# Key and query scratch with the two rows of a map side by side

## The chip, the cores and the metric

The kernel runs on one core of a Trainium2 chip. The metric is the device time of one execution in microseconds (us). The profile shows a single execution, with the instructions of five engines: TensorE (PE, with its weight loads as PEld), VectorE (DVE), ScalarE (ACT), GpSimd (POOL) and SyncE (SP). SP computes nothing here. It issues nearly all transfers between memory and the chip's buffers (DMAs), in one order; ACT issues the weight loads of some stages. The transfers themselves run on the core's 16 DMA engines.

## The reference

Two layers, each with a mixer of three parallel head groups and a feed-forward part, run over 1024 latent tokens and 128 context tokens (1152 columns in all; the keys of the cache add 128). The change touches one of the head groups, the differential attention with 4 heads of two maps each:

```python
def block(qi):
    s = jnp.einsum('bqhmd,bkhmd->bhmqk', qi, k).astype(jnp.float32) * scale
    p = jax.nn.softmax(s, axis=-1)
    w = p[:, :, 0] - lam * p[:, :, 1]
    return jnp.einsum('bhqk,bkhe->bqhe', w.astype(v.dtype), v)
```

The other two groups, a gated DeltaNet and an mLSTM, are recurrences over chunks of the sequence, in both directions. Queries and keys of the latent tokens go through a rotary embedding, in which a pair of channels (x0, x1) becomes (x0 cos - x1 sin, x0 sin + x1 cos).

## The kernel before

Activations lie with channels on the 128 partitions and tokens along the rows, in three groups of 384 columns. Everything is float32; a number is split into a rounded part and a rest (h and l), and a product is three matmuls (`mm3`, L189 to L191), in the attention's scores two (L1250).

Each layer has three stages. In **w_in** the input projections run and their results go to scratch in memory (`open_s`, L430 on). `blk_a` computes queries and keys: two projection blocks, p = 0 and p = 1, hold the first and the second channel of all rotary pairs, 4 maps x 32 channels on the partitions. After the rotary step `put` splits the result in h and l and stores it, by `put_q` in QD and by `put_k` in KD. Beside it `prep1`, `inverse` and `prep2` prepare the recurrences (`prep2` loads ND by the tile w, L851, and stores into RD from X, L911).

In **mixers** the attention (`attention`, L1211 on) and the two recurrences (`scan`) are interleaved on all engines. For each head the attention loads two K tiles, one for a map, 128 partitions x 1280 columns (L1228), and V (L1231). A K tile holds on its partitions h and l of both channels of the pairs: (h or l, p, 32 channels). For each 256 queries it loads one Q tile (L1236) by two DMAs, one for each half of the partitions, because the queries are needed against h and against l of the keys. Then L1250 multiplies (two matmuls into a PSUM bank, for the h and the l part of the queries), L1251 scales and takes the maximum on DVE, L1256 takes the exponential on ACT. K has three buffers, V and Q two. The recurrences load rd, vr, qk, rm, v1 and cq for each step (L1051 to L1149). All these loads are issued by SP, in one order, which the framework that builds the program arranges, with the instructions of all engines, by a simulated timeline; on the chip each engine then works through its own list in order. So a DMA issue that is held up holds up all issues behind it, of the recurrences too.

The third stage is the output projection and the feed-forward part; its weights are loaded by ACT. No line of it is changed.

The layout of the scratch decides what a DMA looks like from the memory's side. Before, QD is `[8, 2, 64, NT]` (map, h or l, 32p + channel, token) and KD is `[2, 2, 2, P, NT + P]` (half, h or l, p, 4 maps x 32 channels, token). A store into QD takes 4 maps x 32 channels, so its outer loop counts 4, and h and l are two DMAs. A load of K takes (h or l, p) x 32 channels, so its outer loop counts 4 too.

Of the kernel before, what the change touches and what calls it, by code (L numbers as in the profile page):

```python
# [9 lines left out]
F32 = mybir.dt.float32  # L10
# [7 lines left out]
P = 128  # L18
# [4 lines left out]
NT = NL + NC  # L23
# [47 lines left out]
class Kern:  # L71
# [362 lines left out]
    def open_s(self, l):  # L434

        S = self.S = {}
        dt = lambda n, shape: self.dr.tile(shape, F32, name=f"{n}{l}")
        S["BT"] = dt("BT", [P, 6, CVO])
        S["CQK"] = dt("CQK", [P, 4, NT])
        S["V1"] = dt("V1", [NCH, P, H, 65])  # L440
        S["BC"] = dt("BC", [NCH, P, 512])
        S["QD"] = dt("QD", [8, 2, 64, NT])
        S["KD"] = dt("KD", [2, 2, 2, P, NT + P])
        S["VD"] = dt("VD", [10, P, 512])
        S["ND"] = dt("ND", [2, NCH, P, H, P])
        S["RD"] = dt("RD", [2, NCH, P, 1024])
        S["GR"] = dt("GR", [2, 16, NT])
        S["VK"] = dt("VK", [NCH, P, 768])
        S["RM"] = dt("RM", [2, NCH, P, 768])
        S["CAT"] = dt("CAT", [KB, P, NT])  # L450
        ed, pe = ExitStack(), ExitStack()
        self.dn = ed.enter_context(self.pool("psdn", PSUM))
        self.pp = pe.enter_context(self.pool("pspp", PSUM))
        return ed, pe
# [472 lines left out]
    def put(self, dst, src, w):  # L927

        t = self.t(self.pr, [P, 2, GW], "kh", 2, F32R)[:, :, :w]
        self.nc.scalar.copy(t[:, 0], src)  # L930
        self.nc.vector.tensor_sub(t[:, 1], src, t[:, 0].bitcast(F32))
        if len(dst) == 1:
            self.nc.sync.dma_start(dst[0], t.bitcast(F32))
        else:
            for i in range(2):
                self.nc.sync.dma_start(dst[i], t[:, i].bitcast(F32))

    def put_k(self, hf, p, cols, src, w):
        self.put([self.S["KD"][hf, :, p, :, cols].rearrange("l r t -> r l t")], src, w)

    def put_q(self, hf, p, cols, src, w):
        self.put([self.S["QD"][4 * hf:4 * hf + 4, hl, 32 * p:32 * p + 32, cols] for hl in range(2)], src, w)

    def blk_a(self, l, qk, hf, u):

# [265 lines left out]
    def attention(self, l):  # L1211

        nc, S, at, pa = self.nc, self.S, self.at, self.pa
# [9 lines left out]
        for h in range(H):  # L1223
            K = []
            for m in range(2):
                k = self.t(at, [P, NT + P], "K", 3, F32R)
                r = 64 * (h % 2) + 32 * m
                nc.sync.dma_start(k.bitcast(F32), S["KD"][h // 2].rearrange("l p r t -> (l p) r t")[:, r:r + 32, :])  # L1228
                K.append(k)
            V = self.t(at, [P, 10, 128], "V", 2)  # L1230
            nc.sync.dma_start(V, S["VD"][:, :, 128 * h:128 * h + 128].rearrange("s p e -> p s e"))  # L1231
            for q0 in range(0, NT, 256):
                nq = min(256, NT - q0)
                q = self.t(at, [P, 2, 2, 256], "Q", 2, F32R)
                for hh in range(2):
                    nc.sync.dma_start(q[64 * hh:64 * hh + 64, :, :, :nq].bitcast(F32), S["QD"][2 * h:2 * h + 2, :, :, q0:q0 + nq].rearrange("m l p t -> p m l t"))  # L1236
                ctx = q0 >= NL
                kt = [9] if ctx else list(range(9))
                groups = [kt] if ctx else [kt[0:3], kt[3:6], kt[6:9]]
# [1 line left out]
                for j in range(nq // 128):  # L1241
                    es, zs = [], []
                    for m in range(2):
                        e = self.t(at, [P, NT], "e", 4)
                        mx = self.t(at, [P, 4], "mx", 4)
                        for i, ks in enumerate(groups):
                            w = 128 * len(ks)
                            p = self.ps(pa, "s", 2)
# [24 lines left out]
                    for i, ks in enumerate(groups):  # L1273
                        n = len(ks)
                        p = self.ps(pa, "t", 1)
# [278 lines left out]
```

## Time and profile before

| | |
|---|---|
| median of 3 runs | 3792.35 us (3791.3 to 3798.47) |
| the profiled execution | 3797.68 us |
| its span, first to last instruction | 3795.9 us, 59415 instructions |
| mean granted TensorE clock in it | 0.954 of full speed |
| DVE, ACT, POOL busy | 2295.8, 1136.6, 654.4 us |
| moved by DMA | 434.13 MB, 277091 packets |

Busy time is the time in which an engine has an instruction of its own under way. A busy PE can still be waiting inside the pipeline, so it is not PE at its peak; but an idle PE is idle. The view of waits tells, for each engine and line, how long the engine was idle just before it, how often, and what released it. The timeline gives instructions in order of time; in it, a bracket holds the idle time of the engine before the instruction and the releaser. Times count from the start of the span. The first layer's mixers run from about 547 to 955 us, the second layer's from about 2425 to 2830 us.

### The profile page before, as it was taken

The page shows a single profiled execution, that of the slowest core. Times are in us where ns is not written, and L with a number is a line of the kernel's source. Part 1 is how long each engine was busy: PE and PEld are TensorE (multiplying, and loading weights), DVE is VectorE, ACT ScalarE, POOL GpSimd, SP SyncE. Part 2 cuts the span into 40 slices and gives each one's busy share as a digit, 9 for nine tenths or more (in the row PEclk, how much of TensorE's full clock was granted, in tenths as well). Part 3 has the DMA queues.
Part 4 walks back from the last instruction along what each step waited for, and adds up shares of the span by engine and source line. Part 5 has one row for each costly group of instructions (what it writes and reads, how often), then busy time and mean ns, then how long its engine had stood idle before and what let it go on. Part 6 is the DMA issues. An engine that isn't in the chain of part 4 may idle for free. (4 is left out here: it accounts for less than half of the span.)

```text
span 3795.9 us, 59415 instructions
## 1 busy us (share of the span) xinstructions
PE 3540.6 (93%) x22770; PEld 3369.8 (89%) x22770; DVE 2295.8 (60%) x5361; ACT 1136.6 (30%) x2383; POOL 654.4 (17%) x903
## 2 busy tenths in 40 slices
PE   7999978997899999999999997898789999999998
PEld 6997777886899999999989877788778999999997
DVE  7896677787455566654485567477775434333435
ACT  5323315445241111111243431244553311111111
POOL 2014232355020000000020324034632000000001
PEclk8999988999999999999999999889999999999999
DMA  5377624774212222221133663467542111111111
GB/s 215 128 247 234 217 78 124 225 214 132 92 59 84 78 81 81 95 78 48 59 110 99 221 230 97 132 175 205 137 140 66 34 39 41 49 40 39 51 45 56
DMA packets 277091, 434.13 MB, mean 114 GB/s; under 512 B 24648, under 2 KB 186504, under 8 KB 276552
## 3 DMA queue, kind: packets, MB, share of 16 engines
q1 hardware_dynamic: 247576, 324.29, 27.3%
q10 hardware_dynamic: 29232, 106.05, 8.7%
q8 instruction: 180, 2.95, 0.3%
q14 instruction: 103, 0.84, 0.1%
HBM read 315.85 MB, written 114.39 MB: 113 GB/s over the span
## 5 line engine op out<-in xcount | busy, mean ns | idle before, releaser
L362 DVE SCALAR_TENSOR_TENSOR x<-pd,mod,x 128x256 f32<-128x256 f32 (+1 forms) x832 | 405.2, 514 | 597.5 <-PE pd L191 596.3
L183 ACT CAST wh<-wr 128x1024 fp32r<-128x1024 f32 (+1 forms) x219 | 229.1, 1047 | 880.3 <-PE pu L190 462.2
L184 DVE TENSOR_TENSOR wl<-wr,wh 128x1024 fp32r<-128x1024 f32 (+1 forms) x219 | 267.6, 1228 | 173.6 <-ACT wh L183 173.1
L189 PE MATMUL pd<-hh,wh 128*128 128x384 f32 x1056 | 358.8, 340 | 7.3 <-DVE x L362 5.1
L189 PE MATMUL pg<-uh,wh 128*128 128x384 f32 x1056 | 357.2, 338 | 2.6 <-ACT uh L342 2.6
L190 PE MATMUL pg<-ul,wh 128*128 128x384 f32 x1056 | 357.9, 339 | 1.4 <-DVE ul L347 1.4
L299 POOL TENSOR_TENSOR nacc<-nacc,nsq 128x384 f32<-128x384 f32 x48 | 52.1, 1086 | 1769.6 <-issue 1572.7
L190 PE MATMUL pu<-ul,wh 128*128 128x384 f32 x1056 | 355.7, 337 | 0.0
L189 PE MATMUL pu<-uh,wh 128*128 128x384 f32 x1056 | 355.6, 337 | 0.0
L190 PE MATMUL pd<-hl,wh 128*128 128x384 f32 x1056 | 354.9, 336 | 0.0
L191 PE MATMUL pg<-uh,wl 128*128 128x384 f32 x1056 | 354.7, 339 | 0.0
L191 PE MATMUL pd<-hh,wl 128*128 128x384 f32 x1056 | 353.7, 336 | 0.0
L191 PE MATMUL pu<-uh,wl 128*128 128x384 f32 x1056 | 350.7, 337 | 0.0
L189 PE MATMUL dn<-uh,wh 128*128 128x384 f32 x864 | 300.1, 347 | 5.8 <-ACT gw L956 4.4
L190 PE MATMUL dn<-ul,wh 128*128 128x384 f32 x864 | 299.0, 346 | 0.0
L191 PE MATMUL dn<-uh,wl 128*128 128x384 f32 x864 | 298.2, 345 | 0.1
L1250 PE MATMUL s<-K,Q 128*128 128x384 f32 (+1 forms) x800 | 226.3, 393 | 58.6 <-DVE e L1251 23.7
L1251 DVE TENSOR_SCALAR_CACHE_REDUCE e<-s 128x384 f32<-128x384 f32 (+1 forms) x400 | 209.8, 539 | 67.8 <-PE s L1250 64.6
L189 PEld LDWEIGHTS pd<-hh,wh 128*128 128x128 f32 x1056 | 198.4, 188 | 18.6 <-issue 7.7
L189 PE MATMUL dn<-wh,uh 128*128 128x256 f32 (+1 forms) x624 | 186.2, 298 | 26.2 <-DVE gw L558 19.8
L1250 PEld LDWEIGHTS s<-K,Q 128*128 128x128 f32 x800 | 138.3, 207 | 78.8 <-DVE e L1251 39.0
L189 PEld LDWEIGHTS pg<-uh,wh 128*128 128x128 f32 x1056 | 199.5, 189 | 4.5 <-ACT uh L342 2.8
(354 smaller groups left out, 8221.6 us busy)
## 6 DMA issues: line engine op xcount, KB each, us to landing
wr<-in_w_gu_dram ACTq DMA_DIRECT2D x88, 512.0 KB
aw<-in_w_mod_dram SPq DMA_DIRECT2D x96, 256.0 KB
wr<-in_w_dn_dram ACTq DMA_DIRECT2D x44, 512.0 KB
wr<-in_w_st_dram ACTq DMA_DIRECT2D x36, 512.0 KB
rd<-RD SPq DMA_DIRECT2D x36, 512.0 KB
aw<-in_w_mod_dram SPq DMA_DIRECT2D x32, 512.0 KB
Q<-QD SPq DMA_DIRECT2D x64, 256.0 KB
RM<-em SPq DMA_DIRECT2D x36, 384.0 KB
```

The source lines that it names most:

```text
L183: nc.scalar.copy(hi, r)
L184: (eng or nc.vector).tensor_tensor(out=lo, in0=r, in1=hi.bitcast(F32), op=ALU.subtract)
L189: mm(out, lhsT=wh, rhs=xh, start=start, stop=False)
L190: mm(out, lhsT=wh, rhs=xl, start=False, stop=False)
L191: mm(out, lhsT=wl, rhs=xh, start=False, stop=stop)
L299: (nc.gpsimd if k in PST else nc.vector).tensor_tensor(out=self.acc[g], in0=self.acc[g], in1=s, op=ALU.add)
L362: nc.vector.scalar_tensor_tensor(out=x[g][k][:, lo:hi], in0=ps[:, lo:hi], scalar=gate[:, k, cnd:cnd + 1], in1=x[g][k][:, lo:hi], op0=ALU.m ...
L1250: nc.tensor.matmul(p[:, :w], lhsT=q[:, m, hl, 128 * j:128 * j + 128], rhs=K[m][:, 128 * ks[0]:128 * ks[0] + w], start=hl == 0, stop=hl == 1)
L1251: nc.vector.tensor_scalar(out=e[:, GW * i:GW * i + w], in0=p[:, :w], scalar1=0.125, scalar2=None, op0=ALU.mult, op1=ALU.max, accum_out=mx[ ...
```

## The change

QD becomes `[2, 2, P, 2, NT]` and KD `[2, 2, P, 2, NT + P]`: half, h or l, 4 maps x 32 channels, p, token. So the two rows of a rotary pair lie next to each other, and the 64 rows of one map are one block. `put` now always issues one DMA with 128 channels as its outer loop, with h and l in it: 24 DMAs into QD instead of 48; the 40 into KD stay. A K tile is loaded by two DMAs, one for h and one for l, of 64 partitions x 1280 columns each: 32 instead of 16. A Q tile is loaded by four DMAs of 64 partitions x (2 maps x 256 columns) each instead of two of twice the size: 160 instead of 80. The order of channels on the partitions of K and Q changes alike. The bytes moved are the same, the issuing engine (SP) too. No instruction of PE, DVE, ACT or POOL is added or removed.

```diff
-        S["QD"] = dt("QD", [8, 2, 64, NT])
-        S["KD"] = dt("KD", [2, 2, 2, P, NT + P])
+        S["QD"] = dt("QD", [2, 2, P, 2, NT])
+        S["KD"] = dt("KD", [2, 2, P, 2, NT + P])
...
-        if len(dst) == 1:
-            self.nc.sync.dma_start(dst[0], t.bitcast(F32))
-        else:
-            for i in range(2):
-                self.nc.sync.dma_start(dst[i], t[:, i].bitcast(F32))
+        self.nc.sync.dma_start(dst.rearrange("l r t -> r l t"), t.bitcast(F32))
 
     def put_k(self, hf, p, cols, src, w):
-        self.put([self.S["KD"][hf, :, p, :, cols].rearrange("l r t -> r l t")], src, w)
+        self.put(self.S["KD"][hf, :, :, p, cols], src, w)
 
     def put_q(self, hf, p, cols, src, w):
-        self.put([self.S["QD"][4 * hf:4 * hf + 4, hl, 32 * p:32 * p + 32, cols] for hl in range(2)], src, w)
+        self.put(self.S["QD"][hf, :, :, p, cols], src, w)
...
-                nc.sync.dma_start(k.bitcast(F32), S["KD"][h // 2].rearrange("l p r t -> (l p) r t")[:, r:r + 32, :])
+                for lk in range(2):
+                    nc.sync.dma_start(k[64 * lk:64 * lk + 64].bitcast(F32), S["KD"][h // 2, lk, r:r + 32].rearrange("r p t -> (r p) t"))
...
+            r0 = 64 * (h % 2)
...
                 for hh in range(2):
-                    nc.sync.dma_start(q[64 * hh:64 * hh + 64, :, :, :nq].bitcast(F32), S["QD"][2 * h:2 * h + 2, :, :, q0:q0 + nq].rearrange("m l p t -> p m l t"))
+                    for hl in range(2):
+                        nc.sync.dma_start(q[64 * hh:64 * hh + 64, :, hl, :nq].bitcast(F32),
+                                     S["QD"][h // 2, hl, r0:r0 + 64, :, q0:q0 + nq].rearrange("(m r) p t -> (r p) m t", m=2))
```

## Rows read from the trace of the kernel before

**Rows 1.** The page, part 1: busy us (share of the span) xinstructions of each engine

```profile
PE 3540.6 (93%) x22770; PEld 3369.8 (89%) x22770; DVE 2295.8 (60%) x5361; ACT 1136.6 (30%) x2383; POOL 654.4 (17%) x903
```

**Rows 2.** PE's waits, 540 to 960 us: us in total, times, longest

```profile
PE s L1250 <- DMA K<-KD: 16.8, 3, 9.0
...
PE s L1250 <- DMA Q<-QD: 6.9, 2, 6.0
...
PE px L893 <- DVE qs L881: 4.1, 1, 4.1
...
PE z L1067 <- DMA qk<-BT: 0.3, 1, 0.3
```

**Rows 3.** PE's waits, 2420 to 2830 us

```profile
PE px L879 <- DMA w<-ND: 13.2, 3, 8.6
PE s L1250 <- DMA Q<-QD: 10.6, 2, 7.9
PE y L1143 <- DMA rm<-RM: 5.5, 1, 5.5
```

**Rows 4.** PE's waits in w_in, 250 to 540, then 2190 to 2320 us

```profile
PE dn L189 <- ACT gw L956: 4.4, 3, 3.0
PE pp L771 <- DMA c<-CQK: 4.3, 2, 3.8
...
PE dn L189 <- ACT gw L956: 5.5, 1, 5.5
```

**Rows 5.** Timeline, first layer's first K: start us, us, line op out<-in [idle before <-releaser]

```profile
548.68 0.55 SPq L1228 DMA_DIRECT2D K<-KD  x1
...
550.04 14.62 SPq L1236 DMA_DIRECT2D Q<-QD  x2
...
572.86 1.62 PE L1250 MATMUL s<-K,Q 128*128 128x384 f32 x4 [9.04 <-DMA K<-KD]
```

**Rows 6.** Timeline, the next head's K in the first layer

```profile
651.67 0.55 SPq L1228 DMA_DIRECT2D K<-KD  x1
652.27 2.54 SPq L1236 DMA_DIRECT2D Q<-QD  x3
...
665.03 1.30 PE L1250 MATMUL s<-K,Q 128*128 128x384 f32 x3 [6.01 <-DMA Q<-QD]
```

**Rows 7.** Timeline of SP, just behind the second layer's first two K

```profile
2431.37 12.13 SPq L851 DMA_DIRECT2D w<-ND  x1
```

**Rows 8.** DMA view, 651 to 667 us, 40 slices: share of 16 engines in tenths, GB/s

```profile
DMA  0005497235899999998532222228899722232222
GB/s 0 0 0 72 110 338 207 64 59 110 225 297 312 236 207 151 197 128 120 97 92 64 90 77 90 102 97 317 341 379 392 259 92 97 95 90 51 46 67 77
```

**Rows 9.** Busy time in stretches: columns, then two stretches (w_in, second layer's mixers)

```profile
core 0: us, PE busy (x) PEld busy (x) DVE busy (x) ACT busy (x) POOL busy (x), PEclk, DMA share, GB/s
290.00:294.00 4.00, 4.00 (x25) 4.00 (x24) 4.00 (x5) 1.00 (x2) 3.37 (x3) 1.00 0.26 79
...
2440.00:2445.00 5.00, 0.00 (x0) 0.00 (x0) 0.00 (x0) 0.00 (x0) 0.00 (x0) 0.50 0.38 117
```

**Rows 10.** The same for 50 us stretches, first layer's mixers

```profile
550.00:600.00 50.00, 33.34 (x341) 28.00 (x337) 23.54 (x78) 16.75 (x46) 3.51 (x4) 0.52 0.60 156
...
750.00:800.00 50.00, 43.55 (x349) 43.21 (x348) 32.38 (x112) 17.52 (x42) 19.04 (x28) 0.93 0.88 250
```

**Rows 11.** DMA issues by line: count, ns min/median/max of one issue, first and last start

```profile
L1228 SPq DMA_DIRECT2D K<-KD x16: 536/557/2634, 547.0 to 2741.2; - x16
...
L1236 SPq DMA_DIRECT2D Q<-QD x80: 573/598/13964, 550.0 to 2805.1; - x80
L936 SPq DMA_DIRECT2D QD<-kh x48: 503/564/2581, 286.9 to 2299.1; - x48
...
L933 SPq DMA_DIRECT2D KD<-kh x40: 359/410/1103, 83.3 to 2259.1; - x40
...
L1014 SPq DMA_DIRECT2D S<-in_s_dram x8: 533/594/601, 685.0 to 2510.3; - x8
```

## Prediction

> **What bounds the kernel now.** I read the engines' busy times first. PE is busy 93% of the span [rows 1], so whatever takes no idle time from PE, and speeds up no instruction of it, can give nothing: 3795.9 - 3540.6 = 255 us of idle PE is all that there is to win. The next view is who ended PE's waits, for the stretches that use the changed scratch. In the first layer's mixers PE waited 16.8 us for K, 6.9 for Q and 4.1 for px [rows 2]; in the second layer's 13.2 for w, 10.6 for Q and 5.5 for rm [rows 3]. In w_in it waited 4.3 us for c and 4.4 + 5.5 us for ACT's gw [rows 4]. Some of these tiles (w, rm, c) are not touched by the change, so the next question is what their loads stood behind.
>
> The timeline tells it. The first K is issued at 547.0 [rows 11] and the second at 548.7; SP then needs 14.6 us for two Q issues, where one takes 0.6 undisturbed, and PE gets to s at 572.9, after 9.0 us of idleness [rows 5, 11]. In the second layer the issue of a w load, right behind two K loads, is held 12.1 us [rows 7]. At 651.7 another K goes out, three Q behind it, and PE waits 6.0 us for Q until 665.0 [rows 6]. So everything behind a K on SP's queue is late, whatever it loads.
>
> The DMA view tells why. In the slices in which nothing else is under way the share of busy engines is 2 tenths, and 90 to 102 GB/s move; in the best slices it is 9, and 379 to 392 GB/s move [rows 8]. While only QD stores are under way the share is 0.26 and the rate 79 GB/s [rows 9]. Four of 16 engines would be 0.25. Four is also the count of the outer loop of both the K load and the QD store on the memory's side. I conclude that these two DMAs, and no others of weight, run on four engines, and that a DMA issued behind them is complete only when its part on those four engines is.
>
> [...]
>
> **The change, part by part.** The sums are made against the profiled execution, 3797.7 us, of which 3795.9 are span and 1.8 lie around it; it is 5.3 us above the median, so I carry the difference over to 3792.4.
>
> K loads. A tile is 128 x 1280 x 4 B = 655 kB: at 97 GB/s 6.8 us, at 385 GB/s 1.7 us [rows 8]. Each of 16 loads thus holds the four engines 5.1 us less, 10.2 us for the two of a head. What this is worth is read from the waits. First layer: the 9.0 us wait for K goes, since the queue in front of it is 10.2 us shorter, and so does px's 4.1, which stands behind the same two loads. The other 7.8 us for K fall into a stretch in which the DMA engines are busy to 0.88 [rows 10]; there bytes count too, and I take half, 3.9. Of the 6.9 for Q, one K stands in front: 5.1 saved, and I leave 1.5. That is 9.0 + 4.1 + 3.9 + 5.4 = 22.4 us. Second layer: of 13.2 for w I leave 2 (the queue is 10.2 us shorter and SP's own 12.1 us hold goes with it); of 10.6 for Q two separate waits, the longer 7.9, lose 5.1 and 1.7; of 5.5 for rm half. That is 11.2 + 6.8 + 2.8 = 20.8 us.
>
> QD stores. 197 kB at 97 GB/s are 2.0 us, at 385 GB/s 0.5: for the old 48 stores 73 us less of the four engines in w_in. Of the 14.2 us of waits there [rows 4] I take half, 7 us: c's load stands behind these stores, for gw I have only that ACT does its casts for QD and KD in between, and both halves are possible. Bounds: 0 and 14.2.
>
> Sum: 22.4 + 20.8 + 7.0 = 50 us. Do they pass to the end? In the long waits all engines stand: between 2440 and 2445 PE, DVE, ACT and POOL are all at 0.00 [rows 9], so nothing else gets done in that time that would have to be done later. But the mixers have a second set of chains, and in the 50 us after the first K, DVE is busy for only 23.5 us and ACT for 16.8 [rows 10], with waits of their own. I take four fifths: 40 us. What is late next is DVE's e behind PE's s, and the recurrences' own chain.
>
> Issues added on SP. Q: 80 more at 0.598 us = 47.8 us, at the old median, since the halves keep 64 partitions; a load with 64 partitions and little data costs as much (S, 0.594). K: 16 more at 0.557 = 8.9. QD: 48 x 0.564 go, 24 x 0.410 come (the price of KD's stores, of the same form), -17.2 [rows 11]. In the mixers 56.7 us more, in w_in 17 less, of two layers together. I cost them at nothing: Q has two buffers and is loaded a block ahead, and PE waited only 0.3 us for a recurrence load in the whole first layer [rows 2]. If that cover is gone, all 56.7 us are on the path; that is the upper end. Below nothing is excluded: issues do not speed up anything.
>
> The clock. [...] I take 0 and for the range up to 16 us in each layer.
>
> The sum: 3792.4 - 40 = 3752 us.
>
> **Rivals.** (1) SP becomes the bound of the scan. Its place is the stretch in which Q, K and the recurrences' loads share the queue; its price 56.7 us, against 40 won: 3792 + 17 = 3809 us. It decides from the point where 40 / 56.7 = 70% of the added issue time delays a load that PE then waits for. For it: rm was waited for already [rows 3]. Against it: 0.3 us for qk [rows 2], and those waits stand behind K loads, which get shorter.
>
> [...]
>
> (2) The gain is absorbed: the stall goes and another chain ends the mixers at the same time, or the order that the framework arranges anew costs as much as is won. Time 3790. For it: only DVE and the recurrences are known to lie close behind; against it: the rows in which all engines stand still.
>
> (3) The change does not do what it says: K's halves still run on few engines, and only QD's stores are spread. Then 7 x 0.8 = 6 us are left: 3787. For it: the issue of a K takes 0.557 us, like those of all 64-partition loads, and not 0.410 like that of KD's store [rows 11]; perhaps a long issue marks few engines. Against it: the shares of 2 tenths follow K alone [rows 6, 8].
>
> (4) More than the forecast: all 27.8 + 29.3 + 14.2 = 71 us of waits go, and some of the clock: 3715.
>
> **How the numbers follow.** Forecast, 3752 with its own range of 3725 to 3780: 0.62. Rival 1: 0.11, rival 2: 0.09, rival 3: 0.08, case 4: 0.10. A difference of 0.2%, 7.6 us, is about what a measurement of this kernel tells from no change. So faster 0.62 + 0.10 = 0.72, same 0.09 + 0.08 = 0.17, slower 0.11. The range goes from 3712 (all waits and a few us of clock) to 3792, which takes in rivals 2 and 3 and leaves out rival 1 and a little at each end.
>
> **What would show it.** Right: while K is loaded the DMA share reads 8 or 9 tenths and the tails of 2 tenths are gone; PE's waits for K, for w and for px are under 3 us in each layer; no issue on SP is held 12 us behind a K; the QD stores number 24 and take 0.41 us to issue. Wrong: shares of 2 tenths with K loads under way (rival 3); PE waiting for rd, vr, qk, rm or v1 for tens of us (rival 1); PE's waits for DMA gone and its idle time the same, for DVE or ACT (rival 2). The prediction falls, above all, if the waits go and the mixers take as long as before.

## The result, and the profile after

The changed kernel takes 3690.5 us (median of 4 runs, 3688.9 to 3694.3), the kernel before 3795.4 beside it (4 runs): a ratio of 0.9725, 95% interval 0.9708 to 0.9742. That is 105 us less where I had forecast 40, and below the range. The profiled execution of after took 3690.3 us, its span is 3688.5 us, its mean granted clock 0.969.

First the page's busy time, against [rows 1], and PE's waits for DMAs in the first layer's mixers, then in the second's, against [rows 2, 3]:

```profile
PE 3517.3 (95%) x22770; PEld 3345.0 (91%) x22770; DVE 2296.8 (62%) x5361; ACT 1133.3 (31%) x2383; POOL 662.7 (18%) x903
```

```profile
PE s L1250 <- DMA Q<-QD: 5.1, 4, 1.9
...
PE y L1139 <- DMA rm<-RM: 1.1, 1, 1.1
```

```profile
PE s L1250 <- DMA Q<-QD: 7.0, 3, 3.1
...
PE z L1063 <- DMA qk<-BT: 1.4, 1, 1.4
```

No wait for K or w is left in either list, and no wait for a DMA is longer than 3.1 us. PE's idle time fell from 255 to 171 us (3688.5 - 3517.3), and its busy time by 23 us, with the same 22770 matmuls: the work itself ran faster too.

The issues on SP (count, ns min/median/max, first and last start), against [rows 11], and the DMA view from 526 to 542 us (busy share of the 16 DMA engines in tenths, and GB/s, in 40 slices), in which the first four halves of K are issued (526.7 to 530.2) and loaded, against [rows 8]:

```profile
L1225 SPq DMA_DIRECT2D K<-KD x32: 450/546/1079, 526.7 to 2644.9; - x32
...
L1235 SPq DMA_DIRECT2D Q<-QD x160: 573/599/1730, 534.3 to 2700.3; - x160
...
L932 SPq DMA_DIRECT2D QD<-kh x24: 360/416/1192, 289.2 to 2226.1; - x24
```

```profile
DMA  9700297979999654799999999999999999999999
GB/s 369 282 10 0 38 205 141 307 205 348 376 238 174 166 166 179 230 284 218 243 307 223 236 205 220 245 213 232 268 278 306 312 312 305 248 314 371 412 355 337
```

Single issues cost what I had said (0.546, 0.599, 0.416 us). What is new is the largest one: no Q issue is held longer than 1.7 us, where it was 14.0 us. The tail of 2 tenths behind K is gone here: from the fifth slice on, 29 of 36 slices read 9 tenths, one reads 2.

Where did the time go? The stages, of before and then of after, in the columns of [rows 9]. They are w_in up to the first px matmul (from 250 us on in the first layer; in the second from the same matmul of PE's list, at 2190.0 and 2137.1 us), then the mixers up to the first pg matmul, for each layer.

```profile
250.00:529.50 279.50, 256.51 (x1561) 225.00 (x1559) 211.71 (x414) 82.97 (x224) 100.16 (x167) 0.93 0.58 192
529.50:1074.80 545.30, 469.26 (x3797) 432.40 (x3796) 370.90 (x1153) 237.50 (x558) 183.50 (x225) 0.91 0.50 148
2190.00:2347.60 157.60, 132.38 (x776) 117.05 (x774) 119.96 (x249) 41.73 (x110) 66.72 (x112) 0.90 0.52 166
2347.60:2937.10 589.50, 517.13 (x4178) 481.42 (x4178) 385.46 (x1174) 240.22 (x567) 181.38 (x225) 0.91 0.50 142
```

```profile
250.00:507.10 257.10, 242.73 (x1542) 214.37 (x1541) 210.63 (x412) 80.46 (x218) 101.82 (x167) 0.98 0.61 208
507.10:1023.50 516.40, 471.71 (x3819) 430.73 (x3819) 375.11 (x1156) 238.30 (x564) 185.10 (x225) 0.94 0.53 156
2137.10:2276.30 139.20, 125.43 (x775) 111.48 (x773) 118.46 (x246) 41.41 (x110) 70.70 (x112) 0.96 0.52 179
2276.30:2829.10 552.80, 511.56 (x4179) 474.83 (x4179) 385.69 (x1174) 239.53 (x567) 182.22 (x225) 0.94 0.51 151
```

w_in got 22.4 and 18.4 us shorter, the mixers 28.9 and 36.7; together 106.4 us, against 107.4 between the spans. Stage length less PE's busy time is its idle time: 196.6 us before, 114.1 after, so 82.5 us of the gain are idle time, and 23.9 us are PE's own time, at a granted clock that rose by 3 to 6 hundredths in every stage.

### The profile page after: what moved, and what is told of

It reads as the page before. It is cut to its first block, busy times and chain, and to the rows that moved or that the text cites. A ratio compares the mean times of both kernels' runs of the same rounds, so it can differ in the third digit from the quotient of the medians.

```text
span 3688.5 us, 59491 instructions
## 1 busy us (share of the span) xinstructions
PE 3517.3 (95%) x22770; PEld 3345.0 (91%) x22770; DVE 2296.8 (62%) x5361; ACT 1133.3 (31%) x2383; POOL 662.7 (18%) x903
## 4 chain that ended last, share of the span: by engine, by line
PE 78%; DVE 10%; DMA 5%; issue 3%; ACT 2%; POOL 1%; SPq 1%; ACTq 0%; POOLq 0%; DVEq 0%
PE pd L189 7%; PE pd L190 6%; PE pd L191 6%; PE pg L191 5%; PE pu L190 5%; PE pu L191 5%; PE pu L189 5%; PE pg L190 5%; PE pg L189 5%; PE dn L189 5%; PE dn L190 5%; PE dn L191 5%; PE s L1250 3%; PE o L1284 2%; DMA Q<-QD 1%
## 5 line engine op out<-in xcount | busy, mean ns | idle before, releaser
L385 DVE TENSOR_TENSOR hs<-pu,hs 128x384 f32<-128x384 f32 x132 | 73.1, 554 | 208.5 <-PE pu L191 201.7
L191 PEld LDWEIGHTS pg<-uh,wl 128*128 128x128 f32 x1056 | 199.1, 189 | 3.8
```

The costliest lines, as they stand in the source:

```text
L191: mm(out, lhsT=wl, rhs=xh, start=False, stop=stop)
L385: nc.vector.tensor_mul(s, pu[:, :GW], s)
```

## The experiments

The change also rearranges the instructions of all engines, since the framework's simulated timeline counts with the new DMAs: only 3767 of DVE's 5361 instructions are the same at the same place of its list. So there are two theories of the gain: **A**, the transfers' own time on the chip, and **B**, the new order. To tell them apart, some kernels have the order of one version, and the access patterns of another written into their DMAs after the order was fixed. The two stages are taken one by one: QD's stores (e1 to e4), then K's loads (e5, e6, e9, e10), then the number and form of the loads on SP (e7, e8, e11, e12). All were timed against the kernel before on their chip ("own order" is the order that the framework arranged for that program; "on 4" and "on 16" name what a program's patterns were written for, and the share of the DMA engines is shown for before, after, e1, e2 and e5 alone):

| kernel | us, median | kernel before | ratio, 95% interval |
|---|---|---|---|
| after | 3690.5 | 3795.4 | 0.9725, 0.9708 to 0.9742 |
| e1 QD on 4 engines, own order | 3741.2 | 3793.2 | 0.9864, 0.9843 to 0.9886 |
| e2 e1's order, QD on 16 | 3700.9 | 3793.2 | 0.9758, 0.9737 to 0.9779 |
| e3 two QD stores on 16, own order | 3702.7 | 3793.2 | 0.9764, 0.9741 to 0.9786 |
| e4 e3's order, QD on 4 | 3742.4 | 3793.2 | 0.9869, 0.9844 to 0.9894 |
| e5 after's order, K on 4 | 3773.6 | 3792.7 | 0.9944, 0.9929 to 0.9959 |
| e6 before, K on 16 | 3746.1 | 3792.7 | 0.9873, 0.9858 to 0.9889 |
| e7 K by one load | 3674.9 | 3792.7 | 0.9685, 0.9667 to 0.9703 |
| e8 Q by eight loads | 3724.9 | 3792.7 | 0.9816, 0.9793 to 0.9839 |
| e9 K on 4, own order | 3774.3 | 3794.5 | 0.9952, 0.9935 to 0.9969 |
| e10 e3's order, QD and K on 4 | 3825.9 | 3794.5 | 1.0087, 1.0071 to 1.0102 |
| e11 Q by two loads | 3706.1 | 3794.5 | 0.9771, 0.9751 to 0.9791 |
| e12 e7, Q into whole tiles | 3674.3 | 3794.5 | 0.9686, 0.9666 to 0.9705 |

### QD's stores: e1 to e4

e1, against after:

```diff
-        S["QD"] = dt("QD", [2, 2, P, 2, NT])
+        S["QD"] = dt("QD", [2, 2, 4, 33, 2, NT])
...
-        self.nc.sync.dma_start(dst.rearrange("l r t -> r l t"), t.bitcast(F32))
+        if len(dst.shape) == 3:
+            self.nc.sync.dma_start(dst.rearrange("l r t -> r l t"), t.bitcast(F32))
+        else:
+            for i in range(2):
+                self.nc.sync.dma_start(dst[i], t[:, i].bitcast(F32))
...
-        self.put(self.S["QD"][hf, :, :, p, cols], src, w)
+        self.put(self.S["QD"][hf, :, :, 0:32, p, cols], src, w)
...
```

> The changed kernel with one part undone: the stores of QD are again two DMAs a block on four engines (the maps of QD lie in four groups of 33, the last of each unused); K, Q and the rest load as in the changed kernel. The w_in stages were 22 and 21 us shorter after the change, the mixers 62 us. Both theories (A: the stores' own time on the chip, B: the order of the instructions that the framework arranges for stores on sixteen engines) expect the 43 us of w_in to go: 3733 us. If it comes out near 3698, my first reckoning of 7 us for the stores was right, and the gain in w_in has another source.

e2, against e1 (the patterns of stores into QD, in a loop over the finished program; Q's loads get the matching addresses):

```diff
...
+                if "QD" in o.memref:
+                    L[j] = copy.replace(i, outs=[copy.replace(o, ap=[[2 * NT, P], [1, GW]], offset=at(o.offset))],
+                                        ins=[copy.replace(s, ap=[[2 * GW, P], [1, GW]])])
...
```

> The program of e1, instruction for instruction in the same order on every engine, but the stores of QD reach 128 maps without gaps, so that each lies on sixteen engines. Theory A (the stores' time on the chip): near the changed kernel, 3690 to 3698 us, and the low clock inside w_in gone. Theory B (the order): as e1, 3733 us.

e3, against after (only QD's stores pass `cols`; the lines on `dge_precook` were not tried by themselves, and e2 has the same stores without them):

```diff
-        self.nc.sync.dma_start(dst.rearrange("l r t -> r l t"), t.bitcast(F32))
+        if cols is None:
+            self.nc.sync.dma_start(dst.rearrange("l r t -> r l t"), t.bitcast(F32))
+        else:
+            for i in range(2):
+                self.nc.dge_precook = False
+                self.nc.sync.dma_start(dst[i], t[:, i].bitcast(F32))
+                self.nc.dge_precook = True
...
-        self.put(self.S["QD"][hf, :, :, p, cols], src, w)
+        self.put(self.S["QD"][hf, :, :, p, cols], src, w, cols)
```

> The changed kernel, with QD stored by two DMAs of 128 maps a block (one for h, one for l) where it has one; each on sixteen engines. The base for e4: both theories 3690 to 3700 us; 24 more issues on SP in w_in at 0.4 to 0.6 us each are 10 to 14 us of SP that nothing in w_in waits for.

e4, against e3:

```diff
...
+                if "QD" in o.memref:
+                    L[j] = copy.replace(i, outs=[copy.replace(o, ap=[[64 * NT, 4], [2 * NT, 32], [1, GW]])],
+                                        ins=[copy.replace(s, ap=[[2 * GW, P], [1, 1], [1, GW]])])
```

> The program of e3 in its order, but each of the two stores of QD a block lies on four engines. Theory A (the stores' time on the chip): w_in loses its 43 us again, 3733 us or more. Theory B (the order): as e3, 3690 to 3700 us.

**Measured.** Engines at the same order: e1 - e2 = 40.3 us, e4 - e3 = 39.7. So theory A holds for QD's stores. The two pairs were meant to have two orders, but they don't: in their traces e1 and e3 have the same 22770 matmuls on PE and the same 1377 DMA issues on SP, one by one. The framework arranged the same order for stores on four engines as for stores on sixteen. So e3 and e4 repeat e1 and e2, to within 2 us, and they say nothing about B. The second store a block, with the order that came with it, cost 10 to 15 us (e2 and e3 against after). I had put it at nothing; where it lies is not shown.

e1 and e2 run the same list of instructions, so the lag of one behind the other can be read for each of them. On PE (start in e1, start in e2, lag, idle time just before it in each):

```
  286.7   283.1    3.6   dn    1.28 / 0.98
  309.0   302.4    6.6   pp    2.27 / 0
  319.4   308.2   11.3   dn    0    / 0
  385.5   372.2   13.3   pp    0.95 / 0
  403.1   386.5   16.6   dn    2.01 / 0
  417.4   395.9   21.5   pp    2.18 / 0
  482.3   459.8   22.5   dn    0    / 0
 1053.6  1033.6   20.0   pu    0    / 0
 2160.8  2138.0   22.8   pp    1.23 / 0
 2257.4  2219.7   37.7   dn    5.50 / 0
 2416.8  2377.0   39.8   s     1.71 / 0.77
 3717.7  3676.1   41.6   pd    0    / 0
```

A lag of 3.6 us is there before the first QD store (288.6 us in e1). Nearly all of the rest grows while QD's stores run (288.6 to 405.4 and 2145.5 to 2271.0 us) and just behind them, and next to nothing of it is ever made good: the lag never shrinks by more than 4.3 us. Between 309.0 and 319.4 it grows by 4.7 us without a pause in e1's list: there PE is slow. The stretch in e1, the one with the same 48 matmuls in e2, and PE's timeline in e1 ahead of it:

```profile
304.00:321.00 17.00, 14.70 (x48) 11.06 (x47) 8.46 (x19) 4.37 (x12) 3.41 (x8) 0.51 0.57 187
```

```profile
299.70:309.00 9.30, 9.30 (x48) 7.63 (x47) 7.74 (x18) 4.14 (x12) 2.77 (x7) 0.83 0.90 309
```

```profile
303.33 0.44 PE L189 MATMUL dn<-uh,wh 128*128 128x384 f32 x1 [3.83 <-ACT gw L956]
309.00 0.69 PE L771 MATMUL pp<-con,c 128*128 128x128 f32 x2 [2.27 <-DMA c<-CQK]
```

In e1 there are two pauses, 3.83 and 2.27 us, and a granted clock of 0.51 for 17 us. In e2 there is one pause, of 2.96 us. Matmuls get slower behind it too: dn, 128x384, takes 0.52 us from 299.5 to 302.4 us, as in e1's slow stretch. But the eight matmuls from cv into pp at 302.9 take 1.13 us, where e1's take 2.08, and most dn take 0.33 to 0.34 us from 305.6 on. The mean clock is 0.83, and the same 48 matmuls take 9.3 us. The DMA view of e1 shows what its transfers do meanwhile, from 289 to 310 us:

```profile
DMA  9722222122223122268422222699758522224998
GB/s 319 287 59 41 79 88 76 38 59 53 73 97 70 53 79 102 97 205 280 162 99 97 106 66 82 149 289 320 287 197 285 169 82 94 99 91 124 310 310 249
```

Now PE's waits in w_in, both layers, e1 first (250 to 530, 2136 to 2320), then e2 (247 to 508, 2110 to 2281):

```profile
PE dn L189 <- DVE gw L558: 7.9, 5, 2.2
PE dn L189 <- ACT gw L956: 5.6, 3, 3.8
PE pp L771 <- DMA c<-CQK: 5.3, 3, 2.3
PE dn L190 <- DVE wl L184: 3.4, 1, 3.4
PE pp L793 <- DVE em L775: 1.7, 2, 1.0
...
PE dn L189 <- DVE gw L558: 9.9, 5, 4.7
PE pp L793 <- DVE em L775: 6.5, 2, 3.7
PE dn L189 <- ACT gw L956: 5.5, 1, 5.5
PE dn L190 <- DVE wl L184: 1.3, 1, 1.3
PE pp L771 <- DMA c<-CQK: 1.2, 1, 1.2
```

```profile
PE dn L189 <- DVE gw L558: 6.2, 4, 2.2
PE dn L189 <- ACT gw L956: 4.4, 3, 3.0
PE dn L190 <- DVE wl L184: 3.8, 2, 3.3
...
PE dn L189 <- DVE gw L558: 10.8, 4, 5.2
PE dn L190 <- DVE wl L184: 1.4, 1, 1.4
```

23.9 + 24.4 us against 14.4 + 12.2: 21.7 us of waits less, for 40.3 us of time. The time is not made up of waits alone: over the whole span PE is busy for 3537.1 us in e1 and for 3514.1 in e2, with the same matmuls. So 23.0 of the 40.3 us are PE's own slower time, and 17.3 us are idle time. Of the waits, only 6.5 us name a DMA. ACT's gw of 5.5 us in the second layer waited for a QD store by the view of e1's stores, and em (8.2 us) stands behind a store of RM on the same queue, as DVE's own waits in the first layer tell, e1's and then e2's:

```profile
DVE em L775 <- DMA RM<-em: 17.7, 7, 4.2
```

```profile
DVE em L775 <- DMA RM<-em: 6.5, 5, 1.8
```

### K's loads: e5, e6, e9, e10

e5, against after:

```diff
...
+                if "KD" in s.memref:
+                    L[j] = copy.replace(i, outs=[copy.replace(o, ap=[[NT + P, 64], [1, 1], [1, NT + P]])],
+                                        ins=[copy.replace(s, ap=[[16 * (NT + P), 4], [NT + P, 16], [1, NT + P]])])
```

> The changed kernel in its own order, but the loads of K's halves lie on four engines, as before the change (32 loads; Q's loads and QD's stores untouched). Theory A (the transfers' time on the chip): K is late again by the 9 to 16.8 us of the first map of each mixer, and what is queued behind it with it: 20 to 40 us above the changed kernel, 3710 to 3730 us. Theory B (the order): the mixers' gain came from the rearranged order, so within 10 us of the changed kernel, 3690 to 3700 us.

e6, against before:

```diff
-                nc.sync.dma_start(k.bitcast(F32), S["KD"][h // 2].rearrange("l p r t -> (l p) r t")[:, r:r + 32, :])
+                for a in range(4):
+                    nc.sync.dma_start(k[32 * a:32 * a + 32].bitcast(F32), S["KD"][h // 2, a // 2, a % 2, r:r + 32, :])
```

> The kernel before, with one part of the change's effect done alone: K is loaded by four DMAs of 32 partitions on sixteen engines where it was two on four; QD's layout, stores and loads as before. Theory A: the first K of each layer comes 9 to 17 us sooner, and w in layer 1 as well; 20 to 40 us below the kernel before, 3755 to 3775 us. Theory B: the order up to the mixer is that of before, so what is gained is what the mixers' rearranged order gives, at most 10 us: 3785 to 3795 us.

e9, against after:

```diff
-        S["KD"] = dt("KD", [2, 2, P, 2, NT + P])
+        S["KD"] = dt("KD", [2, 2, 16, 9, 2, NT + P])
...
-                r = 64 * (h % 2) + 32 * m
+                r = 8 * (h % 2) + 4 * m
...
-                    nc.sync.dma_start(k[64 * lk:64 * lk + 64].bitcast(F32), S["KD"][h // 2, lk, r:r + 32].rearrange("r p t -> (r p) t"))
+                    nc.sync.dma_start(k[64 * lk:64 * lk + 64].bitcast(F32), S["KD"][h // 2, lk, r:r + 4, 0:8].rearrange("a r p t -> a (r p) t"))
```

Not shown: KD's stores go to the same 8 rows of 9, and are two DMAs a block here (80 where after has 40).

> The changed kernel with the rows of KD in groups of 8 maps with a gap, so that the loads of K's halves lie on four engines and the framework arranges all instructions for that (in e5 they kept the order arranged for loads on sixteen; KD's stores are two a block here). If K's time on the chip is all, as e5: 3774 us. If the order has its share, so that an order made for a late K hides part of it: down to the time of the kernel before less the 41 us of the QD stores, 3752 us.

e10 is e3's program with the patterns of e4 and of e5.

> The program of e3 in its order, with both of the change's effects undone on the chip: QD's stores and K's loads lie on four engines. If the two costs are separate (w_in and the mixers): 3703 + 40 + 83 = 3826 us, which is slower than the kernel before by 33 us, the price of four loads of Q a block and of an order made for early transfers. If one stage's pauses cover the other's: 3790 to 3800 us.

**Measured.** K on four engines costs 83 us at after's order (e5), and 83.5 at e4's (e10 - e4). So A was right in kind; but my own number for it, 20 to 40 us, was less than half. e9, in an order of its own, takes 3774.3 where e5 takes 3773.6. But e9 has 40 more stores of KD, and what these cost is not known, so the order's share is not isolated there. e10 came out where the sum of the single costs puts it, 3825.9 for 3826: the two costs lie in different stages and don't cover each other.

What e10 settles is theory B. It has the change's loads and a new order, but K and QD on four engines as before, and it is 31 us slower than the kernel before. From there the engines alone, at the same order, are worth 123.2 us (e10 - e3), and one QD store a block in place of two, with the order that comes with it, 12.2 (e3 - after). Together that is a gain of -31 + 123 + 12 = 104 us, where 105 were measured. So the gain is the engines' time, and the added loads and the new order together took some of it back. Which of those two did is not shown.

e6, K alone from the kernel before, gave 46.6 us, above both expectations. Why K is worth 47 us from before (e6) and 83 from after (e5) was not tried by itself. It fits that after has 160 loads of Q where before has 80, and that PE waited 35.2 us for Q in e5 and 17.4 in before; that this is the cause is not shown.

PE's waits for DMAs in e5's mixers, first layer (507 to 1070 us) and second (2324 to 2912), to be read against those of after above:

```profile
PE s L1250 <- DMA Q<-QD: 16.3, 3, 8.1
...
PE px L879 <- DMA w<-ND: 7.7, 1, 7.7
...
PE s L1250 <- DMA K<-KD: 5.7, 1, 5.7
PE s L1250 <- DMA w<-ND: 3.7, 1, 3.7
PE y L1139 <- DMA rm<-RM: 3.4, 1, 3.4
```

```profile
PE s L1250 <- DMA Q<-QD: 18.9, 4, 6.8
...
PE y L1139 <- DMA rm<-RM: 4.3, 1, 4.3
...
PE s L1250 <- DMA K<-KD: 3.6, 1, 3.6
...
PE px L879 <- DMA w<-ND: 2.0, 1, 2.0
...
PE z L1063 <- DMA qk<-BT: 1.0, 1, 1.0
```

36.8 + 29.8 us, against 6.2 + 8.4 in after: 52 us of waits for DMAs, for 83 us of time. Between the mixers of the two profiles lie 81 us: 65 us are idle time of PE, the 52 among them, and 16 are its own time, at a granted clock of 0.91 and 0.92 for 0.94. The lag of e5 behind after, read as for e1 and e2, is 0.6 us before the first K and 83.0 at the end; it never shrinks by more than 6.7 us. Most of the waits are booked to Q and w, as before the change. The queue shows why. SP in e5 behind the first K, and the DMA view from 526 to 558 us:

```profile
535.31 11.69 SPq L1235 DMA_DIRECT2D Q<-QD  x1
```

```profile
DMA  8605823226994899972222222227987776228969
GB/s 315 251 0 128 294 87 91 96 64 119 358 271 97 225 161 181 147 138 64 100 90 102 102 109 106 83 95 223 307 318 179 180 216 190 91 91 238 270 209 338
```

The long hold, the share of 2 tenths and the 64 to 109 GB/s beside it are back, and with them the waits. e1 against e2, and e5 against after, change the outer count on the memory's side at the same order. With a count of four, 21 of e1's 40 slices above and 14 of e5's read 2 tenths (four of 16 engines would be 0.25). With e2's 128 over the same 21 us (285 to 306) two single slices read 2 tenths and 16 read 8 or 9, at up to 427 GB/s; with after's halves (526 to 558) no slice reads 2, and 34 of 40 read 8 or 9. So here a count of four goes with about four engines; what a count of another size would give is not shown.

### Number and form of the loads: e7, e8, e11, e12

e7, against after:

```diff
-        S["KD"] = dt("KD", [2, 2, P, 2, NT + P])
+        S["KD"] = dt("KD", [2, P, 2, 2, NT + P])
...
-        self.put(self.S["KD"][hf, :, :, p, cols], src, w)
+        self.put(self.S["KD"][hf, :, p, :, cols].rearrange("r l t -> l r t"), src, w)
...
-                for lk in range(2):
-                    nc.sync.dma_start(k[64 * lk:64 * lk + 64].bitcast(F32), S["KD"][h // 2, lk, r:r + 32].rearrange("r p t -> (r p) t"))
+                nc.sync.dma_start(k.bitcast(F32), S["KD"][h // 2, r:r + 32].rearrange("r p l t -> (r p l) t"))
...
-                        nc.sync.dma_start(q[64 * hh:64 * hh + 64, :, hl, :nq].bitcast(F32),
+                        nc.sync.dma_start(q[hh:128:2, :, hl, :nq].bitcast(F32),
```

> The changed kernel with K's two halves in adjacent rows of KD, so that one DMA of 128 rows loads a K (16 loads where there are 32); Q goes to every second partition. [...] If K is hidden now, 3690 us within 4.

e12, against e7:

```diff
-                for hh in range(2):
+                for m in range(2):
                     for hl in range(2):
-                        nc.sync.dma_start(q[hh:128:2, :, hl, :nq].bitcast(F32),
-                                     S["QD"][h // 2, hl, r0:r0 + 64, :, q0:q0 + nq].rearrange("(m r) p t -> (r p) m t", m=2))
+                        src = S["QD"][h // 2, hl, r0 + 32 * m:r0 + 32 * m + 32, :, q0:q0 + nq].rearrange("r p t -> (r p) t")
+                        nc.sync.dma_start(q[:, m, hl, :nq].bitcast(F32), src.unsqueeze(1).to_broadcast([64, 2, nq]))
```

> e7 (K by one load), with Q still by four loads a block, but each writes all 128 partitions of half the columns (it reads its 64 rows twice) where it wrote 64 partitions of all. Same count, same bytes. If loads into halves of the partitions are what cost e7's 16 us, another 5 to 15 us go: 3660 to 3670 us. If it was the number of loads or K's place in the queue: 3675 us within 5.

e8, against after:

```diff
-                        nc.sync.dma_start(q[64 * hh:64 * hh + 64, :, hl, :nq].bitcast(F32),
-                                     S["QD"][h // 2, hl, r0:r0 + 64, :, q0:q0 + nq].rearrange("(m r) p t -> (r p) m t", m=2))
+                        for m in range(2):
+                            nc.sync.dma_start(q[64 * hh:64 * hh + 64, m, hl, :nq].bitcast(F32),
+                                         S["QD"][h // 2, hl, r0 + 32 * m:r0 + 32 * m + 32, :, q0:q0 + nq].rearrange("r p t -> (r p) t"))
```

> The changed kernel with Q loaded by eight DMAs a block in place of four: 160 more issues on SP, at 0.41 us each 66 us of SP inside the mixers. My rival in which SP becomes the bound of the scan: some 66 us more, 3756 us. If SP has room there, as my forecast took it, under 5 us more: 3690 to 3696 us.

e11, against after (Q keeps the channel order of the kernel before and K has that of after, so it leaves out the right pairing of channels in the scores; instructions and sizes are those of a full run):

```diff
-        S["QD"] = dt("QD", [2, 2, P, 2, NT])
+        S["QD"] = dt("QD", [8, 2, 64, NT])
...
+            for i in range(4):
+                self.nc.sync.dma_start(dst[i], t[32 * i:32 * i + 32].bitcast(F32))
...
-        self.put(self.S["QD"][hf, :, :, p, cols], src, w)
+        self.put([self.S["QD"][4 * hf + i, :, 32 * p:32 * p + 32, cols].rearrange("l r t -> r l t") for i in range(4)], src, w)
...
-                    for hl in range(2):
-                        nc.sync.dma_start(q[64 * hh:64 * hh + 64, :, hl, :nq].bitcast(F32),
-                                     S["QD"][h // 2, hl, r0:r0 + 64, :, q0:q0 + nq].rearrange("(m r) p t -> (r p) m t", m=2))
+                    nc.sync.dma_start(q[64 * hh:64 * hh + 64, :, :, :nq].bitcast(F32), S["QD"][2 * h:2 * h + 2, :, :, q0:q0 + nq].rearrange("m l p t -> p m l t"))
```

> The changed kernel with the maps of QD as in the kernel before, stored by four DMAs of 32 maps a block (each on sixteen engines) and loaded by two DMAs a block in place of four: 80 issues fewer in the mixers, 72 more in w_in. By e8, where 160 more issues cost 34 us, 80 fewer give up to 17 us: 3673 us; by e3, where 24 more stores cost 12 us, 72 more in w_in cost up to 36 us: 3709 to 3727 us. If the issues on SP are covered in both stages: 3690 us within 5.

**Measured.** e7, with e12 beside it, beats both kernels: 3674.9, 13 to 16 us below after, where I had 3690 within 4 if K is hidden. In e7's second layer the mixers took 537.5 us (first px at 2273.8, first pg at 2811.3) where after took 552.8, and PE's wait for Q is down to one of 1.3 us:

```profile
PE s L1249 <- DMA Q<-QD: 1.3, 1, 1.3
```

e12 tells what it was not: Q into whole tiles, at the same count, is 3674.3, the same, each in its own order. For Q whole against half makes no difference here; for K one load in place of two goes with 13 to 16 us, but in e7 the count of issues and the order change with it, and which of the three it is stays open.

e8, 160 issues more, is 34 to 37 us slower than after. All issues of Q together take 182.6 us in e8 and 100.0 in after, so this is less than half of the added 82.6. In the profiled run, the slowest of the four, the first layer's mixers paid 2.6 us for their 80 issues, the second's 35.5 (519.0 and 588.3 us, by the starts of px and pg). So added issues did cost time, as rival 1 has it. What the change's own 96 issues cost is not isolated; it is part of the 31 us of e10. What SP waited for in e8's second mixers (2380 to 2800 us) and in after's (2373 to 2730):

```profile
SPq L1236 <- PE s L1251: 62.0, 9, 22.5
```

```profile
SPq L1235 <- PE s L1250: 20.3, 5, 8.4
```

SP stood 62 us, up to 22.5 at a time, until PE gave a Q buffer free, with the recurrences' loads queued behind that. e11 went the other way, 80 issues fewer in the mixers and 72 more in w_in, and lost 16 us against after; it doesn't tell the two apart.

## Why the prediction was wrong

The sum had the mixers' waits right and the wrong price for them, and it had w_in's waits wrong. Of the 66 us that the stages gained beyond it, 35 lie in w_in and 31 in the mixers.

| stage | waits I let go | waits that went | time I forecast (x 4/5) | time that went |
|---|---|---|---|---|
| mixers, layer 0 | 22.4 | 28.1 - 6.2 = 21.9 | 17.9 | 28.9 |
| mixers, layer 1 | 20.8 | 29.3 - 8.4 = 20.9 | 16.6 | 36.7 |
| w_in, both | 7.0 | 20.1 | 5.6 | 40.8 |

(The waits that went are those for K, Q, px, w, rm and qk of [rows 2, 3] less those of after; for w_in, which has waits of many names, PE's idle time of the stages, 48.2 - 28.1.)

**Right.** Four engines, and the queue behind them: with K or QD on four the share reads 2 tenths (e1, e5), and a Q issue behind K is held up to 11.7 us in e5, 1.7 at most in after. That a DMA behind such a transfer is complete only when its part on those engines is was my conclusion; no view shows single engines. The 1.7 us for a K and 0.5 for a QD store, at the 385 GB/s of [rows 8], were my estimate for the changed forms, and no run shows the time of one such transfer; what after showed in its place is a mean of 247 GB/s over the 16 us in which its first K are loaded, beside other transfers. The waits in the mixers: 43.2 us forecast, 42.8 gone. That the sums lie so near is luck in part: K's waits went whole (16.8, where I had let 12.9 go) and w's too (13.2 for 11.2), while Q's fell by 5.4 where I had let 12.2 go. All four signs listed for "right" are there.

**Not shown: issues on SP at nothing.** The mixers' waits went although SP issued 96 more loads there. The durations of all DMA issues on SP in the two mixers sum to 349 us before and 343 after, so the holds that disappeared were worth as much as the issues that came. But e10, with K and QD on four engines again, is 31 us slower than the kernel before, by the added issues or by the order; so this term may have been hidden behind a larger gain.

**Wrong, first step: "I take four fifths".** Next to no pause of PE was made good: the lag shrinks by at most 4.3 us between e1 and e2 and by 6.7 between after and e5. It is even more than one for one: at the same order 52 us of waits for DMAs cost 83 us (e5), 21.7 us of waits 40.3 (e1). I had argued that other chains would take up the slack since DVE and ACT are idle half the time. But PE is busy for 93%, and the pause is PE's; I read it so that slack on engines that don't bound the time buys nothing. The surplus has two parts. One is PE's own slower time (16 us between e5 and after in the mixers, 23.0 between e1 and e2). The other is idle time that names no DMA: between before and after PE's idle time in the mixers fell by 62.5 us, of which 42.8 name a DMA or px. Among the rest are waits booked to DVE's e; that they follow from PE's own lateness is likely, not shown.

**Wrong, second step: "The clock. I take 0".** In the four stages PE's own time fell by 23.9 us, at a granted clock of 0.94 to 0.98 for 0.90 to 0.93. 20.7 of it lie in w_in, 3.1 in the mixers (some twenty matmuls moved from the one to the other in the first layer). [Rows 10] had the low clock, 0.52, behind the first K, with PE busy for 33.3 us. The 16 us a layer in my range are 33.3 x (1 - 0.52), an estimate of what a full clock would have saved there. No run shows them; what the runs showed in their place is the 3.1 us of the mixers of both layers. That place still has a low clock after the change, though PE is busy for 47.2 of 50 us:

```profile
525.00:575.00 50.00, 47.20 (x538) 40.71 (x536) 32.65 (x110) 22.27 (x63) 3.69 (x4) 0.62 0.72 195
```

The gain lay mainly in w_in, where I had looked for none; e1 against e2 shows it there, with 23.0 us of PE's own time for the stores' engines alone.

**Wrong, third step: the term of w_in, 7 us.** I took half of the 14.2 us of [rows 4]. Of these, c's 4.3 and the second layer's gw of 5.5 went, but the first layer's gw of 4.4 stayed:

```profile
PE dn L189 <- ACT gw L952: 4.4, 3, 2.9
```

The rest of the 20.1 us was in lines that I had left out of [rows 4]: em (7.7 us in both layers, gone) and DVE's gw (19.8, now 15.0). Only c names a DMA: em waited for a store of RM on the same queue, as the DVE rows of e1 and e2 show. A wait booked to an engine must be followed one step further, to what that engine waited for. And half of what w_in gained was no wait at all, but PE's own time.

**Two readings.** The 90 to 102 GB/s that I gave for slices at 2 tenths are the upper part; [rows 8] has 46 to 102 there. And Q's term in the first layer takes off 5.4 us, where the 5.1 saved beside it would leave 1.8 and not 1.5. Neither changes the sum by much.

**The rivals.** (1) SP as the bound fell as a whole: the time went down by 105 us. That its price was nothing is not shown (e8, e10). (2) Absorbed or reordered fell too: the gain was not taken back, and e10 shows that the order and the added loads together cost 31 us while the transfers stay on four engines. (3) K's halves are not held to few engines (share 9 tenths in after, where before read 2). (4) All 71 us of waits and some of the clock, 3715, was the nearest; it was still 25 us high, since the clock in w_in and the waits behind em were in none of my cases.

## What to carry over

On the engine that bounds the kernel (here PE, busy for 93%), count each pause at its full length, add its slow time after it from a row that shows the granted clock (0.52 in [rows 10]), and expect next to nothing of it to be caught up: here the lag never shrank by more than 4.3 of 40 us (e1) and 6.7 of 83 (e5). Follow waits that name an engine one step further: here DMAs on few engines delayed what was issued behind them, stores too, and showed up under the names of others (DVE's em waited 17.7 us for stores of RM in e1's first layer, 6.5 in e2's). When layout and order change together, fix the order and change the access pattern alone: here that priced the engines at 40 and 83 us. And compare the lists of two runs before you call them two orders: e1 and e3 had the same.

## What the runs showed of the hardware that I had not expected

- Few engines cost far more here than the waits that name the transfer: 48 stores of QD, with 6.5 us of waits that name a DMA, 40 us (e1 against e2); 32 halves of K, with 9.3 us of waits that name K, 83 us (e5 against after).
- In e1, with a pause of 3.8 us and another of 2.3 us soon behind it, TensorE was granted 0.51 over 17 us; in e2 the same 48 matmuls, after a single pause of 3.0 us, ran at 0.83, in 9.3 us. What went ahead of the low clock is shown, its cause is not.
- The costs of K and of QD on four engines, in different stages, added up in e10, within what its runs differ by (3826 expected, 3825.9 measured, 3824.0 to 3828.7).
- 160 issues more on SP's queue cost 2.6 us in the first layer's mixers and nearly half a microsecond each in the second's (35.5 us for 80), in the one profiled run of e8.
